# Weight splits of a decoder layer: low blocks 160 columns apart, low products placed first, second or last by block, the up projection's first high block 64 bytes up, and branch sums with a PSUM operand

## The chip, the cores and the metric

The kernel runs on one core of a Trainium2 chip. The metric is the device time of one execution in microseconds; lower is better. The kernel before took 432.97 us (median of 3 runs, 432.74 to 433.79). A core has TensorE for matrix products (PE in the profile, with its weight loads listed apart as PEld), VectorE (DVE), ScalarE (ACT), GpSimd (POOL) and SyncE (SP, which here only starts transfers). Operands lie in an on-chip memory of 128 partitions (SBUF), and TensorE writes its sums to eight banks of PSUM.

## The reference

One layer of a causal decoder for 256 tokens of width 1024, in float32. Three attention mixers (A: sparse with an indexer, B: dilated windows, C: blocks) share one input projection. Then their outputs are gated and merged, and a feed-forward block follows:

```python
gates = sigmoid(x @ w_gate).reshape(bsz, s_len, 3, D_MODEL)
merged = (gates[:, :, 0] * (o_a @ w_br_a)
          + gates[:, :, 1] * (o_b @ w_br_b)
          + gates[:, :, 2] * (o_c @ w_br_c))
x = layer_norm(ALPHA * x + merged @ w_out, ln1_g, ln1_b)
h = square(relu(x @ w_up)) @ w_down
ple = sigmoid(x @ w_ple_gate) * (p @ w_ple)
x = layer_norm(ALPHA * x + h + ple, ln2_g, ln2_b)
```

## The kernel before, in words

**Three products for one.** Every weight block and every activation is held as a pair: a high part rounded to the type fp32r, and a low part, which is the rest. A product of 128 by 128 weights with an activation is made of three matmuls into the same sum: high weight with high activation, high weight with low activation, low weight with high activation. `prod` (L154) issues them. Its argument `low` says where the matmul with the low weight stands: 0 is first, 1 is second, 2 is last. Each of the three matmuls loads its own weights.

**The stream of weights.** `Weights` (L58) takes all weights in one fixed order of units. A unit is up to 128 by 1024 floats (eight blocks of 128 columns). `_split` (L73) starts its transfer into a `raw` buffer (SP queue), copies it to the high tile `whi` with the rounding (ACT, L86), and subtracts to get the low tile `wlo` (L94). For the first 58 units VectorE makes the first 640 of each 1024 columns of `wlo` and GpSimd the others (`DV`); later VectorE makes all. There are five buffers each of `raw`, `whi` and `wlo`, and `get` (L98) keeps the split four units ahead of its use. `whi` and `wlo` are tiles of 1152 floats, and a unit may lie some columns into its tile: `at` gives the offsets. For gate and feature units the high part begins at column 40; of the low part the first five blocks begin at column 72, and the last three sit 32 columns closer (offset 40). `Apart` (L48) is the view with that one cut; the subtraction is cut at the same column. For the up projection the high part begins at 0, the first low block at 64, the others from 208 on.

**The stages.** First the indexer's features; then features (`feat`, L288), gates (`fill("g")`, L265) and values fill the matrix engine between the steps of attention, one head after the other (`head`, `slots`, `attend`). A gate or feature unit is one `gemm` (L164): 24 matmuls of 256 columns, for the eight blocks k = 0 to 7. There `low` is 2 for k = 0 to 4 and 0, 1, 2 for k = 5, 6, 7. From the last mixer on, `fill("c")` also computes the branch products of mixers B and C from `op`, which holds the attention outputs: five blocks, 15 matmuls of 256 columns, always with the low one last. The sums of both branches lie side by side in one PSUM bank (512 columns); L285 multiplies both by the gates into `G`, and L286 adds the two halves. `freed` names the instruction after which the bank counts as read. Then `merge` (L608) does the A branch: four units `u_ba` of six blocks, low last. Then come the output projection, the first norm with the gate of `p`, the up projection, the down projection and the second norm.

**The up projection.** L837 to L875: 32 units. In each, eight matmuls of 512 columns with the high blocks (L847: high and low activation side by side as one moving operand), then eight of 256 columns with the low blocks (L849). Its results go through a reduction on VectorE (L831), two ScalarE steps and a split.

**The order.** The pool layout puts `xh` and `xl` (the activation of the layer's input), `op`, `x1` (the input of the up projection) and the weight tiles at fixed bytes of each partition. The small tile `gap` (L314) only shifts `op`. The order of instructions on each engine is set when the program is built, by a list scheduler that works with modelled times, and partly by hand (`pin`, `issue_after`, `high_priority`).

Of the kernel before, what the change touches and what calls it, by code (L numbers as in the profile page):

```python
# [11 lines left out]
F32 = mybir.dt.float32  # L12
F32R = mybir.dt.float32r
ALU = mybir.AluOpType
# [25 lines left out]
FIRST = 4  # L40
DV = 640
# [5 lines left out]

class Apart:  # L48

    def __init__(self, t, cut, front, back):  # L50
        self.t, self.cut, self.at = t, cut, (front, back)

    def __getitem__(self, key):
        o = self.at[key[1].start >= self.cut]
        return self.t[:, o + key[1].start:o + key[1].stop]


class Weights:  # L58
# [14 lines left out]
    def _split(self, u):  # L73
        nc = self.nc
        src, n, hi, lo, r, by, _, at = self.units[u]
        if callable(src):
            r = src()
        elif r is None:
            r = self.raw.tile([128, 1024], F32, name="raw", tag="raw")[:, :n]
        if not callable(src):  # L80
            self.loads.append(nc.sync.dma_start(r, src).ins)
        if hi is None:
            hi = self.part.tile([128, 1152], F32R, name="whi", tag="whi")[:, at[0]:at[0] + n]
            lo = self.part.tile([128, 1152], F32R, name="wlo", tag="wlo")
            lo = Apart(lo, *at[2:], at[1]) if len(at) > 2 else lo[:, at[1]:at[1] + n]
        self.copies.append(nc.scalar.copy(hi, r).ins)  # L86
        cut = ((nc.vector, slice(None)),) if by == "v" else (
            (nc.vector, slice(0, by * n // 1024)), (nc.gpsimd, slice(by * n // 1024, n)))
        if len(at) > 2:
            o = at[2]  # L90
            cut = [(e, slice(a, b)) for e, c in cut for a, b in (
                (c.start or 0, min(c.stop or n, o)), (max(c.start or 0, o), c.stop or n)) if a < b]
        for e, c in cut:
            i = e.tensor_tensor(lo[:, c], r[:, c], hi[:, c].bitcast(F32), op=ALU.subtract)  # L94
        self.subs.append(i.ins)
        self.parts[u] = (hi, lo)

# [16 lines left out]
def hybrid_layer(ctx: ExitStack, tc: tile.TileContext, x0, xn, pT, wqk, wva, wvb, wg, wbc, wba,  # L114
                 wout, wup, wdn, wpg, wple, lnrow, rel, onehot, pick, out):
    nc = tc.nc
    pe, act, dve, pool = nc.tensor, nc.scalar, nc.vector, nc.gpsimd
# [9 lines left out]
    W = Weights(tc, raw, part)  # L127
# [20 lines left out]
    t = banks.tile([128, 512], F32, name="b4", tag="b4")  # L148
# [5 lines left out]
    def prod(ps, a, b, first, last, hold=False, more=False, low=2):  # L154

        terms = [(0, 0), (0, 1)]
        terms.insert(low, (1, 0))
        for n, (x, y) in enumerate(terms):
            i = pe.matmul(ps, lhsT=a[x], rhs=b[y], start=first and n == 0, stop=last and n == 2,  # L159
                          skip_group_check=more)  # L160
            if hold and n == 0:
                pin(i)

    def gemm(ps, units, xs, k=0):  # L164

        for u in units:
            hi, lo = W.get(u)
            for o in range(0, hi.shape[1], 128):
                prod(ps, (hi[:, o:o + 128], lo[:, o:o + 128]), xs[k], k == 0, k == len(xs) - 1,
                     low=(k - 5) if k > 4 else 2)  # L170
                k += 1


# [1 line left out]
    pm = mid.enter_context(tc.tile_pool(name="pm", bufs=1))  # L175
    one = ctx.enter_context(ExitStack())
    right = lambda n, b: one.enter_context(tc.tile_pool(name=n, bufs=b, side="right"))
    p1, k1, kp = (right(n, b) for n, b in (("p1", 1), ("k1", 2), ("kp", 3)))
# [3 lines left out]
    xs = [(xh[:, k], xl[:, k]) for k in range(KT)]  # L182
    n_u = [0]

    def add(*a, at=(0, 0)):
        i = n_u[0]
        n_u[0] += 1
        return W.add(*a, by=DV if i < 58 else "v", at=at)

    G = pm.tile([128, 24, S], F32, name="G")  # L190
    u_q = [[] for _ in range(FIRST)]

    u_g, u_bc, u_ba, u_out = [], [], [], []
    for t in TASKS:
        if t == "va":
            u_va = [add(wva[i], 656) for i in range(4)]
        elif t == "vb":
            u_vb = [add(wvb[i], 768, at=(56, 56)) for i in range(4)]
        elif t in "gcao":
            u, w, n = {"g": (u_g, wg, 1024), "c": (u_bc, wbc, 640), "a": (u_ba, wba, 768),  # L200
                       "o": (u_out, wout, 1024)}[t]
            u.append([add(w[len(u)], n, at=(0, 0) if t == "o" else (40, 72, 640, 40) if t == "g" else (40, 40))])
        else:
            u_q.append([add(wqk[int(t) - FIRST], 1024, at=(40, 72, 640, 40))])

    def toeplitz(h0, step):
        t = tp.tile([128, 3, 256], F32, name="T", tag="T")
# [29 lines left out]
    def freed(*ins):  # L237


        if banks_first[0]:  # L240
            W.after = tuple(i.ins for i in ins)
        return ins[0].ins
# [22 lines left out]
    def fill(what):  # L265


        for w in what:
            if w == "g":
                ps = mmbank(256)  # L270
                gemm(ps, u_g[n_g[0]], xs)
                freed(act.activation(G[:, n_g[0]], ps, AF.Tanh, scale=0.5))
                n_g[0] += 1
                continue
            f = n_c[0]
            n_c[0] += 1
            hi, lo = W.get(u_bc[f][0])
            ps = mmbank(512).rearrange("p (i s) -> p i s", i=2)
            for i, (k0, k1) in enumerate(((3, 5), (5, 8))):
                for k in range(k0, k1):  # L280
                    c = slice((k - 3) * 128, (k - 2) * 128)
                    prod(ps[:, i], (hi[:, c], lo[:, c]), (op[:, k, 0], op[:, k, 1]), k == k0,
                         k == k1 - 1)
            g = G[:, 3 * f + 1:3 * f + 3]
            freed(dve.scalar_tensor_tensor(g, g, 1.0, ps, op0=ALU.add, op1=ALU.mult))  # L285
            dve.tensor_tensor(g[:, 0], g[:, 0], g[:, 1], op=ALU.add)  # L286

    def feat(f):  # L288
        ps = mmbank(256)
# [21 lines left out]

    V = p1.tile([128, 2, 11, 128], F32R, name="V")
    iw = p1.tile([128, 2, 8], F32, name="iw")
    pm.tile([128, 24], F32, name="gap")  # L314
    op = pm.tile([128, 8, 2, S], F32R, name="op")

    def values(units, n, h0, heads, withiw):
# [109 lines left out]
    with ExitStack() as begin:  # L427
# [6 lines left out]
        cut = [((0, 384), (384, 768)) if k == 0 else ((0, 768),) for k in range(KT)]  # L434
        with tc.high_priority(offset=1000):
            for k in range(KT):
                for i, (a, b) in enumerate(cut[k]):
                    e = nc.scalar if i else nc.sync
                    e.dma_start(g0[:, k, a:b], x0[k, :, a:b])
            for k in range(KT):  # L440
                act.copy(xh[:, k], g0[:, k, 0:S])
                for a, b in cut[k]:
                    a = max(a, S)
# [12 lines left out]
    ps = feat(4)  # L456
# [37 lines left out]
    for j in range(2):  # L494
        ps = feat(5 + 4 * j)
        k = k_pair(ps)
# [6 lines left out]
        o = opair()  # L503
# [11 lines left out]
    for j in range(3):  # L515
        ps = feat(13 + 2 * j)
        k = k_pair(ps)
        q = q_pair(feat(14 + 2 * j))
        s = logits(k, q)
        o = opair()  # L520
        for h in range(2):
            n = 2 * j + h
# [10 lines left out]
    for j in range(3):  # L533
        s = logits(kA, q)
        o = opair()
        for h in range(2):
            n = 2 * j + h
# [23 lines left out]
    u_out += [add(wout[4 + i], 1024, wo[:, i, 0], wo[:, i, 1]) for i in range(4)]  # L561
    u_ple = [add(wple[i], 1024) for i in range(2)]
    u_pg = [add(wpg[i], 1024) for i in range(8)]
    u_up = [[add(wup[i], 1024, at=(0, 80, 128, 64))] for i in range(32)]

    H = (slice(0, 512), slice(512, 1024))

    class Wide:
# [3 lines left out]
        def __init__(self, units, stat, cut=(H, H)):  # L572
            self.units, self.stat, self.cut, self.ws = units, stat, cut, {}
            self.acc = [[next(ps_a) for _ in H] for _ in range(2)]
# [33 lines left out]
    def merge(p):  # L608
        hi, lo = W.get(u_ba[p][0])
        ps = mmbank(512).rearrange("p (f s) -> p f s", f=2)  # L610
        for f in range(2):
            for k in range(3):
                c = slice((3 * f + k) * 128, (3 * f + k + 1) * 128)
                prod(ps[:, f], (hi[:, c], lo[:, c]), (op[:, k, 0], op[:, k, 1]), k == 0, k == 2)
        g6 = G[:, 6 * p:6 * p + 6].rearrange("p (f i) s -> p f i s", f=2)
        g = g6[:, :, 0]
        dve.scalar_tensor_tensor(g, g, 1.0, ps, op0=ALU.add, op1=ALU.mult)
        dve.tensor_tensor(g, g, g6[:, :, 1], op=ALU.add)
        for f in range(2):
            o = 8192 + 512 * (2 * p + f)  # L620
            m = store[:, o:o + 512].rearrange("p (a s) -> p a s", a=2)
            act.mul(m[:, 0], g[:, f], 0.5)
            dve.scalar_tensor_tensor(m[:, 1], g[:, f], 0.5, m[:, 0].bitcast(F32), op0=ALU.mult,
                                     op1=ALU.subtract)
            mt.append(m)
# [84 lines left out]
    for i in range(4):  # L710
# [3 lines left out]
        b, cs = i // 2, H[i % 2]  # L714
        t = slice(b * 128, (b + 1) * 128)
        ps = mmbank(512)
# [62 lines left out]
    hT, at, room = {}, 0, 0  # L779
    for k in (*SEQ, *LATE):  # L780
        i = PAIRS.index(k) if k in PAIRS else -1
        n = 512 if i < 0 else 1792
        if i in (0, 1):
            t = p2.tile([128, 2048], F32R, name=("X", "PL")[i], tag=("X", "PL")[i])[:, 0:n]
        elif i in (2, 3) or k == 2:
            t = more[:, room:room + n]
            room += n
        else:
            t = store[:, at:at + n]
# [31 lines left out]
    for k in (*SEQ, *LATE):  # L821
        if k in PAIRS:
            i = PAIRS.index(k)
# [13 lines left out]
    for f in range(32):  # L837
# [5 lines left out]
        ps = mmbank(512).rearrange("p (b a t) -> p b a t", b=2, a=2)  # L843
        hi, lo = W.get(u_up[f][0])
# [15 lines left out]
        j = half_of[f].index(f)  # L860
# [47 lines left out]
    for k in SEQ[:-2]:  # L908
# [16 lines left out]
    v = w2.tile([128, D], F32, name="a8", tag="a8")  # L925
# [15 lines left out]
    for i, acc in enumerate(ends):  # L941
        c = slice(256 * i, 256 * i + 256)
# [28 lines left out]
    for b in range(2):  # L971
        t = slice(128 * b, 128 * b + 128)
# [109 lines left out]
```

## Time and profile before

| | |
|---|---|
| median of 3 runs | 432.97 us (432.74 to 433.79) |
| the profiled execution | 433.55 us; span in the trace 431.4 us |
| three kinds of matmul with `xh` or `xl` at L159 | 336 each, 279 to 281 ns from start to end |
| L847 and L849 | 256 each, 392 and 276 ns |
| high copies, L86 on ACT | 124 of raw tiles, 123.3 us |
| low subtractions, L94 | DVE 137.2 us, POOL 76.3 us |

The profile gives the time of one execution seen by the hardware profiler. The duration of a matmul is longer than the distance to the next one, since matmuls run into each other; what counts for TensorE is the distance from start to start. In the chain of waits a row has the start, the length and the number of instructions, so length by count is that distance where nothing else lies between. In the groups of instructions, a row gives busy time and mean duration, then the idle time of the engine before them.

### The profile page before, as it was taken

To read this page: it belongs to the slowest core of one execution; us is meant where nothing else is said; L and a number is where in the kernel's file an instruction comes from. 1 tells how busy PE (TensorE), PEld (TensorE's weight loads), DVE (VectorE), ACT (ScalarE), POOL (GpSimd) and SP (SyncE) were. 2 spreads that over 40 slices of the span, in tenths; PEclk is the share of its full clock that TensorE was granted. 3 is DMA by queue.
4 is the path that set the end of the run, shared out by engine and by line. 5 is a ranking of instruction groups with operands and counts; after the bars stand their busy time and mean duration, and the time that the engine had idled before them with its cause. 6 is when DMAs were issued, how large, how long until landed. Compare 5 with 4: busy or idle time off the path is not lost.

```text
span 431.4 us, 7768 instructions
## 1 busy us (share of the span) xinstructions
PE 420.4 (97%) x2804; PEld 380.4 (88%) x2804; DVE 350.5 (81%) x637; ACT 276.4 (64%) x499; POOL 123.1 (29%) x127
## 2 busy tenths in 40 slices
PE   8999999999999999999999999999999999999993
PEld 8989989999999999999887888888888888888883
DVE  4959967686576689989957878999898789999755
ACT  6777366586787785757605566887788755667310
POOL 1658246365534559400000003222530000000001
PEclk9999999999999999999999999999999999999998
DMA  8895976577554427478860677686576287647402
GB/s 292 300 327 133 257 241 195 165 224 233 161 164 131 129 74 213 121 219 330 276 259 13 216 266 206 191 289 195 173 214 193 65 286 236 183 158 231 159 2 97
DMA packets 28155, 84.28 MB, mean 195 GB/s; under 512 B 2977, under 2 KB 6985, under 8 KB 27733
## 3 DMA queue, kind: packets, MB, share of 16 engines
q1 hardware_dynamic: 26880, 79.54, 57.0%
q10 hardware_dynamic: 1140, 4.19, 3.1%
q8 instruction: 22, 0.36, 0.4%
q14 instruction: 17, 0.13, 0.1%
q0 software_dynamic: 96, 0.06, 0.0%
HBM read 81.88 MB, written 1.90 MB: 194 GB/s over the span
## 4 chain that ended last, share of the span: by engine, by line
PE 79%; DVE 8%; issue 3%; ACT 1%; POOLq 0%; DVEq 0%; POOL 0%
PE mm L159 30%; PE b L159 25%; PE mm L847 14%; PE mm L849 7%; DVE wlo L94 2%; PE b L306 2%; PE b L347 1%; DVE idx L474 1%; PE b L351 1%; DVE idx L484 1%; DVE G L285 1%; DVE G L286 1%; DVE m L483 0%; DVE eb L396 0%; DVE e L375 0%
## 5 line engine op out<-in xcount | busy, mean ns | idle before, releaser
L94 DVE TENSOR_TENSOR wlo<-raw,whi 128x640 fp32r<-128x640 f32 (+7 forms) x156 | 137.2, 903 | 24.0 <-ACT whi L86 21.8
L86 ACT CAST whi<-raw 128x1024 fp32r<-128x1024 f32 (+3 forms) x124 | 123.3, 1003 | 47.9 <-PE b L159 18.3
L94 POOL TENSOR_TENSOR wlo<-raw,whi 128x384 fp32r<-128x384 f32 (+3 forms) x58 | 76.3, 1326 | 78.0 <-ACT whi L86 75.1
L159 PE MATMUL mm<-xh,whi 128*128 128x256 f32 x336 | 92.7, 281 | 0.2 <-DVE k L260 0.2
L159 PE MATMUL mm<-xl,whi 128*128 128x256 f32 x336 | 92.0, 279 | 0.0
L159 PE MATMUL mm<-xh,wlo 128*128 128x256 f32 x336 | 87.4, 280 | 0.0
L159 PEld LDWEIGHTS mm<-xh,whi 128*128 128x128 f32 x336 | 63.1, 188 | 1.1 <-DVE k L260 0.4
L847 PE MATMUL mm<-x,whi 128*128 128x512 f32 x256 | 64.0, 392 | 0.0
L159 PEld LDWEIGHTS mm<-xl,whi 128*128 128x128 f32 x336 | 63.1, 188 | 0.5
L159 PEld LDWEIGHTS mm<-xh,wlo 128*128 128x128 f32 x336 | 60.1, 188 | 0.3
L159 PE MATMUL b<-whi,store 128*128 128x512 f32 x168 | 54.0, 389 | 0.0
L847 PEld LDWEIGHTS mm<-x,whi 128*128 128x128 f32 x256 | 45.8, 188 | 8.3
L664 POOL TENSOR_TENSOR rs<-rs,half 128x1 f32<-128x1 f32 x4 | 3.4, 841 | 147.1 <-DVE rs L663 147.1
L159 PEld LDWEIGHTS b<-whi,store 128*128 128x128 f32 x168 | 31.5, 188 | 6.5
L849 PEld LDWEIGHTS mm<-x,wlo 128*128 128x128 f32 x256 | 33.8, 188 | 2.5
L849 PE MATMUL mm<-x,wlo 128*128 128x256 f32 x256 | 34.3, 276 | 0.0
L159 PE MATMUL b<-wlo,store 128*128 128x512 f32 x84 | 32.7, 390 | 0.0
L159 PE MATMUL mm<-op,whi 128*128 128x256 f32 x128 | 23.4, 283 | 0.0
L870 POOL TENSOR_TENSOR a<-a 128x128 f32<-128x128 f32 x7 | 4.5, 640 | 60.4 <-ACT a L833 54.9
L159 PE MATMUL b<-whi,x 128*128 128x512 f32 x64 | 20.5, 395 | 0.0
L159 PEld LDWEIGHTS mm<-op,whi 128*128 128x128 f32 x128 | 19.6, 189 | 0.4 <-DVE G L285 0.3
L159 PEld LDWEIGHTS b<-wlo,store 128*128 128x128 f32 x84 | 15.8, 188 | 3.3
(219 smaller groups left out, 794.2 us busy)
## 6 DMA issues: line engine op xcount, KB each, us to landing
raw<-in_wup_dram SPq DMA_DIRECT2D x32, 512.0 KB
raw<-in_wg_dram SPq DMA_DIRECT2D x24, 512.0 KB
raw<-in_wqk_dram SPq DMA_DIRECT2D x18, 512.0 KB
raw<-in_wdn_dram SPq DMA_DIRECT2D x18, 512.0 KB
raw<-in_wout_dram SPq DMA_DIRECT2D x8, 512.0 KB
raw<-in_wpg_dram SPq DMA_DIRECT2D x8, 512.0 KB
T<-tabd SPq DMA_DIRECT2D x24, 128.0 KB
xr<-in_wdn_dram SPq DMA_DIRECT2D x6, 512.0 KB
```

Of the source, the lines that this page charges most:

```text
L86: self.copies.append(nc.scalar.copy(hi, r).ins)
L94: i = e.tensor_tensor(lo[:, c], r[:, c], hi[:, c].bitcast(F32), op=ALU.subtract)
L159: i = pe.matmul(ps, lhsT=a[x], rhs=b[y], start=first and n == 0, stop=last and n == 2, skip_group_check=more)
L285: freed(dve.scalar_tensor_tensor(g, g, 1.0, ps, op0=ALU.add, op1=ALU.mult))
L286: dve.tensor_tensor(g[:, 0], g[:, 0], g[:, 1], op=ALU.add)
L306: m = pe.matmul(ss[2 * n + h][:, QC[b]], lhsT=q[d, x, c], rhs=k[d, y, 0:128 * (b + 1)], start=i == 0, stop=i == 2)
L347: pe.transpose(t[:, 128 * i:128 * i + 128], P[:, 128 * i:128 * i + 128], ident)
L351: pe.matmul(v, lhsT=V[:, 0, vh], rhs=pt[:, :, 0:256], start=True, stop=False)
L474: dve.scalar_tensor_tensor(idx[:, QC[1]], r[:, h, QC[1]], iw[:, 1, n:n + 1], idx[:, QC[1]], op0=ALU.mult, op1=ALU.add)
L847: pe.matmul(ps, lhsT=hi[:, c], rhs=x1[:, :, k], start=k == 0, stop=False)
L849: pe.matmul(ps[:, :, 0], lhsT=lo[:, c], rhs=x1[:, :, k, 0], start=False, stop=k == KT - 1)
L870: pool.tensor_tensor(sums[2], a11, a21, op=ALU.subtract)
```

## The change

Low blocks get offsets of their own (tables `LOW` and `UP`), the tiles become 1088 floats for `whi` and 1216 for `wlo` (together as before), and `Apart` becomes a view by a list of offsets. Its `runs` finds stretches with an even step, and each stretch is one instruction with a pattern of blocks of 128 columns. In a gate or feature unit the first five low blocks are 160 columns apart, the last three 128. Branch units of mixers B and C get five blocks at 40, 200, 360, 520 and 648; VectorE makes three of the blocks and GpSimd two (before, 400 and 240 columns). Units of the A branch get six blocks 160 apart. `TURN` says for each block where the low matmul stands. In the up projection the first high block moves to column 16 and the others begin at 192, so the high copy on ACT becomes two instructions (256 and 768 columns), and the low subtraction, two instructions before too (128 and 896), is now cut at 256. `gap` grows by 32 floats. In `fill("c")` the product with the gate is made in two instructions, one for each half; the second mixer's half goes back to PSUM, and the sum then reads one operand from PSUM; the bank is now freed by the sum.

```diff
 class Apart:
-    def __init__(self, t, cut, front, back):
-        self.t, self.cut, self.at = t, cut, (front, back)
+    def __init__(self, t, at):
+        self.t, self.at = t, at
     def __getitem__(self, key):
-        o = self.at[key[1].start >= self.cut]
-        return self.t[:, o + key[1].start:o + key[1].stop]
+        o = self.at[key[1].start // 128]
+        return self.t[:, o:o + 128]
+    def runs(self, a, b):
+        i, end = a // 128, b // 128
+        while i < end:
+            j = i + 1
+            while j < end and self.at[j] - self.at[j - 1] == self.at[i + 1] - self.at[i]:
+                j += 1
+            yield 128 * i, 128 * j
+            i = j
+    def view(self, a, b):
+        i, n = a // 128, (b - a) // 128
+        step = self.at[i + 1] - self.at[i] if n > 1 else 128
+        t = self.t[:, self.at[i]:self.at[i] + n * step]
+        return t.rearrange("p (k c) -> p k c", c=step)[:, :, 0:128]
...
-            hi = self.part.tile([128, 1152], F32R, name="whi", tag="whi")[:, at[0]:at[0] + n]
-            lo = self.part.tile([128, 1152], F32R, name="wlo", tag="wlo")
-            lo = Apart(lo, *at[2:], at[1]) if len(at) > 2 else lo[:, at[1]:at[1] + n]
-        self.copies.append(nc.scalar.copy(hi, r).ins)
+            hi = self.part.tile([128, 1088], F32R, name="whi", tag="whi")
+            lo = self.part.tile([128, 1216], F32R, name="wlo", tag="wlo")
+            hi, lo = (t[:, o:o + n] if isinstance(o, int) else Apart(t, o)
+                      for t, o in zip((hi, lo), at))
+        for a, b in hi.runs(0, n) if isinstance(hi, Apart) else ():
+            i = nc.scalar.copy(blocks(hi, a, b), blocks(r, a, b))
...
+            for x in lo.runs(c0, c1):
+                i = e.tensor_tensor(blocks(lo, *x), blocks(r, *x), blocks(hi, *x).bitcast(F32),
+                                    op=ALU.subtract)
...
-                     low=(k - 5) if k > 4 else 2)
+                     low=TURN["g"][k])
...
+    LOW = {"g": (8, 168, 328, 488, 648, 776, 904, 1032), "c": (40, 200, 360, 520, 648),
+           "a": (40, 200, 360, 520, 680, 840)}
+    TURN = {"g": (0, 2, 1, 2, 2, 0, 1, 2), "c": (2, 0, 2, 1, 2), "a": (2, 1, 2, 2, 2, 0)}
...
-                         k == k1 - 1)
+                         k == k1 - 1, low=TURN["c"][k - 3])
             g = G[:, 3 * f + 1:3 * f + 3]
-            freed(dve.scalar_tensor_tensor(g, g, 1.0, ps, op0=ALU.add, op1=ALU.mult))
-            dve.tensor_tensor(g[:, 0], g[:, 0], g[:, 1], op=ALU.add)
+            for i, o in ((1, ps[:, 1]), (0, g[:, 0])):
+                dve.scalar_tensor_tensor(o, g[:, i], 1.0, ps[:, i], op0=ALU.add, op1=ALU.mult)
+            freed(dve.tensor_tensor(g[:, 0], g[:, 0], ps[:, 1], op=ALU.add))
...
-    pm.tile([128, 24], F32, name="gap")
+    pm.tile([128, 56], F32, name="gap")
...
-    u_up = [[add(wup[i], 1024, at=(0, 80, 128, 64))] for i in range(32)]
+    UP = (16, *range(192, 1088, 128)), (64, *range(208, 1104, 128))
+    u_up = [[add(wup[i], 1024, at=UP)] for i in range(32)]
...
-                prod(ps[:, f], (hi[:, c], lo[:, c]), (op[:, k, 0], op[:, k, 1]), k == 0, k == 2)
+                prod(ps[:, f], (hi[:, c], lo[:, c]), (op[:, k, 0], op[:, k, 1]), k == 0, k == 2,
+                     low=TURN["a"][3 * f + k])
```

More of the change, by code (lines that the diff above doesn't have):

```diff
@@ L48, with blocks @@
 class Apart:
-    def __init__(self, t, cut, front, back):
-        self.t, self.cut, self.at = t, cut, (front, back)
+    def __init__(self, t, at):
+        self.t, self.at = t, at
     def __getitem__(self, key):
-        o = self.at[key[1].start >= self.cut]
-        return self.t[:, o + key[1].start:o + key[1].stop]
+        o = self.at[key[1].start // 128]
[13 more added lines that the diff above has]
+        return t.rearrange("p (k c) -> p k c", c=step)[:, :, 0:128]
+def blocks(t, a, b):
+    return (t.view(a, b) if isinstance(t, Apart) else
+            t[:, a:b].rearrange("p (k c) -> p k c", c=128))
 class Weights:
@@ L82, in _split @@
         if hi is None:
-            hi = self.part.tile([128, 1152], F32R, name="whi", tag="whi")[:, at[0]:at[0] + n]
-            lo = self.part.tile([128, 1152], F32R, name="wlo", tag="wlo")
-            lo = Apart(lo, *at[2:], at[1]) if len(at) > 2 else lo[:, at[1]:at[1] + n]
[L86 to L94, printed above, removed]
+            hi = self.part.tile([128, 1088], F32R, name="whi", tag="whi")
[4 more added lines that the diff above has]
+            i = nc.scalar.copy(blocks(hi, a, b), blocks(r, a, b))
+        if not isinstance(hi, Apart):
+            i = nc.scalar.copy(hi, r)
+        self.copies.append(i.ins)
+        c = n if by == "v" else by * n // 1024
+        for e, c0, c1 in ((nc.vector, 0, c), (nc.gpsimd, c, n)):
+            if not isinstance(lo, Apart):
+                if c0 < c1:
+                    x = slice(c0, c1)
+                    i = e.tensor_tensor(lo[:, x], r[:, x], hi[:, x].bitcast(F32),
+                                        op=ALU.subtract)
+                continue
+            for x in lo.runs(c0, c1):
+                i = e.tensor_tensor(blocks(lo, *x), blocks(r, *x), blocks(hi, *x).bitcast(F32),
+                                    op=ALU.subtract)
         self.subs.append(i.ins)
@@ L183, in hybrid_layer, with add @@
     n_u = [0]
-    def add(*a, at=(0, 0)):
+    def add(*a, at=(0, 0), by=DV):
         i = n_u[0]
         n_u[0] += 1
-        return W.add(*a, by=DV if i < 58 else "v", at=at)
+        return W.add(*a, by=by if i < 58 else "v", at=at)
+    LOW = {"g": (8, 168, 328, 488, 648, 776, 904, 1032), "c": (40, 200, 360, 520, 648),
+           "a": (40, 200, 360, 520, 680, 840)}
+    TURN = {"g": (0, 2, 1, 2, 2, 0, 1, 2), "c": (2, 0, 2, 1, 2), "a": (2, 1, 2, 2, 2, 0)}
     G = pm.tile([128, 24, S], F32, name="G")
@@ L201, in hybrid_layer @@
                        "o": (u_out, wout, 1024)}[t]
-            u.append([add(w[len(u)], n, at=(0, 0) if t == "o" else (40, 72, 640, 40) if t == "g" else (40, 40))])
+            u.append([add(w[len(u)], n, at=(40, LOW[t]) if t in LOW else (0, 0),
+                          by=615 if t == "c" else DV)])
         else:
-            u_q.append([add(wqk[int(t) - FIRST], 1024, at=(40, 72, 640, 40))])
+            u_q.append([add(wqk[int(t) - FIRST], 1024, at=(40, LOW["g"]))])
     def toeplitz(h0, step):
```

## The prediction

> **What bounds the kernel now.** I read the page first (engines, then the chain that ended last), then the chain in order of time, then the starts of TensorE's instructions.
>
> ```profile
> span 431.4 us, 7768 instructions
> PE 420.4 (97%) x2804; PEld 380.4 (88%) x2804; DVE 350.5 (81%) x637; ACT 276.4 (64%) x499; POOL 123.1 (29%) x127
> PEclk9999999999999999999999999999999999999998
> PE 79%; DVE 8%; issue 3%; ACT 1%; POOLq 0%; DVEq 0%; POOL 0%
> ```
>
> TensorE is busy for 97% of the span at the full clock, and 79% of the chain is its own work. So the time is the number of matmuls by the distance from one to the next. The change removes no matmul. It can gain only if that distance, or a wait of TensorE, gets shorter. The distance is not one number:
>
> ```profile
> 77.34 4.08 PE mm L159 x36
> 112.88 4.43 PE mm L159 x39
> 187.62 14.70 PE mm L159 x125
> 253.71 1.81 PE mm L847 x8
> 255.52 0.91 PE mm L849 x8
> 256.43 1.84 PE mm L847 x8
> 258.27 0.91 PE mm L849 x8
> ...
> 338.83 1.84 PE mm L847 x8
> 340.67 0.91 PE mm L849 x8
> ```
>
> All L159 rows here are matmuls of 256 columns at the same clock. 36 in 4.08 us is 113.3 ns each, 39 in 4.43 us is 113.6, but 125 in 14.70 us is 117.6. In the up projection the first unit takes 256.43 - 253.71 = 2.72 us; the other 31 go from 256.43 to 341.58 (340.67 + 0.91), 2.747 us each. The 0.03 us lies in the eight wide matmuls (1.84 for 1.81), none in the narrow ones. So there are two paces, and the starts show where they change:
>
> ```profile
> 29.73 0.28 PE L159 MATMUL mm<-xh,whi 128*128 128x256 f32 x1
> ...
> 42.45 0.28 PE L159 MATMUL mm<-xh,wlo 128*128 128x256 f32 x1
> ...
> 141.81 0.40 PE L159 MATMUL mm<-op,whi 128*128 128x256 f32 x2
> ...
> 189.46 0.28 PE L159 MATMUL mm<-xh,whi 128*128 128x256 f32 x1
> 189.57 0.28 PE L159 MATMUL mm<-xh,wlo 128*128 128x256 f32 x1
> 189.69 0.28 PE L159 MATMUL mm<-xl,whi 128*128 128x256 f32 x1
> ...
> 190.14 0.40 PE L159 MATMUL mm<-op,whi 128*128 128x256 f32 x2
> ...
> 190.73 0.28 PE L159 MATMUL mm<-op,wlo 128*128 128x256 f32 x1
> ...
> 196.03 0.28 PE L159 MATMUL mm<-op,wlo 128*128 128x256 f32 x1
> ...
> 202.03 0.28 PE L159 MATMUL mm<-op,wlo 128*128 128x256 f32 x1
> ```
>
> From 189.46 to 190.14 six steps take 113 ns each; from 190.73 to 196.03 45 steps take 117.8 each. The pace stays as it is until something flips it. I call 113 ns the short step and 117.8 the long step. I went through the starts of all dense steps up to the end of the branch products: of 964 with `xh` or `xl`, 342 take 116 ns or more (first at 29.73, last at 189.46); of 186 with `op`, 140 (first at 141.81, last at 202.03). A long step costs 4.45 ns more (117.83 against 113.38 on average), so 1.5 us and 0.6 us are lost.
>
> What flips it? Eleven times a stretch of long steps reaches block 6 of a `gemm`, where the low matmul stands second (first at 42.45, last at 189.57); ten times it is over two steps later. From short to long it goes at transposes and other products of attention, and at every one of the three entries into `op` that come with short steps (141.81 and 190.14 are the first and the last).
>
> The layout explains the last point. In the program before, all `whi` and `wlo` buffers begin at 192 bytes modulo 256, `xh` and `xl` at 160, `op` at 32, `x1` at 192. A high block (column 40) lies 64 bytes below `xh` and 64 above `op`, modulo 256. The low blocks 0 to 4 lie like the high ones; the blocks 5 to 7, around which long steps end, lie 128 bytes off. Modulo 128 every load of these products is 64 from the moving operand. In the up projection the wide matmuls run at 0 and the narrow ones at 64; the exception is the first high block, which is loaded beside the last narrow matmul at 0. The wide matmuls after it are the longer ones. In the first unit, which comes after wide ones, they aren't.
>
> **The change part by part.** *First high up block.* At column 16 it lies 64 bytes from `x1`, so the load beside a narrow matmul has the distance of all others there, and the load of the next block beside a wide one has 0, as now. If that ends the loss, 31 units lose 27 ns each: 0.83 us. I take 0.8; the lower bound is nothing, and below nothing if the step from 64 to 0 then comes one matmul too early: at most 27 ns again, +0.8 us.
>
> *Order and low blocks.* With the new sizes (4352 and 4864 bytes) all buffers still begin at 192 modulo 256. The new low offsets put blocks 0, 2, 4, 5, 6 and 7 of a gate unit 128 bytes off the high ones, and `TURN` has the low matmul second at blocks 2 and 6, first at 0 and 5. Each of these sits on an offset of the kind at which long steps end now, at 5 and 6. The strong kind (second) comes twice in 24 steps, once before. Then a long stretch that a product of attention has begun lasts some 5 steps, not some 12: an estimate from the places in the cycle. I take 60% of the 342 long steps as gone: 205 by 4.45 ns, 0.9 us. Bounds: 0 to 1.5 us.
>
> *`op` 128 bytes further.* Now it lies to the weights as `xh` does, so the entry has no flip, and `TURN` for the branch units has a second-place low matmul as well. I take 75% of 140: 0.45 us. Bounds: 0 to 0.6 us; the loss below nothing that both edits could bring is the last rival.
>
> The rule that speaks against all this: the Trainium skill, "TensorE: Matmul & The Clock Gate", section "Back-to-back issue gap", makes the warm distance a function of the columns alone (N / 2.4 + 2.5 ns, by which 256 columns are 109 ns, an estimate). The trace disagrees: 113.3 and 117.8. By the rule the sum would be 0.
>
> *The cost on the other engines.*
>
> ```profile
> 254.00:342.00 88.00, 88.00 (x514) 77.25 (x513) 80.15 (x127) 68.55 (x121) 21.63 (x28) 1.00 0.62 187
> ...
> L86 ACT CAST whi<-raw 128x1024 fp32r<-128x1024 f32 x104 | 108.1, 1049 | 47.1 <-PE b L159 18.3 <-PE mm L159 9.2 <-DMA raw<-in_wqk_dram 7.6
> L86 ACT CAST whi<-raw 128x768 fp32r<-128x768 f32 x8 | 6.6, 830 | 0.3 <-issue 0.3
> L360 ACT CAST op<-o 128x256 fp32r<-128x256 f32 x8 | 3.2, 404 | 0.7 <-DVE o L357 0.7
> L249 DVE SCALAR_TENSOR_TENSOR q<-mm,q 128x256 fp32r<-128x256 f32 x12 | 4.9, 411 | 2.7 <-ACT q L248 2.7
> L260 DVE TENSOR_TENSOR k<-mm,k 128x256 fp32r<-128x256 f32 x5 | 2.1, 415 | 0.2
> L285 DVE SCALAR_TENSOR_TENSOR G<-G,mm x8: 669/672/679, 156.6 to 194.5; 128x512 f32<-128x512 f32 x8
> L286 DVE TENSOR_TENSOR G<-G x8: 404/416/1241, 161.0 to 196.2; 128x256 f32<-128x256 f32 x8
> L286 DVE TENSOR_TENSOR G<-G 128x256 f32<-128x256 f32 x8 | 5.1, 639 | 0.0
> L617 DVE SCALAR_TENSOR_TENSOR G<-G,mm 128x512 f32<-128x512 f32 x4 | 2.7, 679 | 0.0
> L703 DVE TENSOR_TENSOR x<-mm,x 128x512 fp32r<-128x512 f32 x3 | 2.0, 688 | 2.4 <-ACT x L699 2.4
> L727 DVE SCALAR_TENSOR_TENSOR b<-Y,PL 128x512 f32<-128x512 f32 x4 | 2.7, 695 | 0.0
> L726 DVE SCALAR_TENSOR_TENSOR PL<-sg,PL 128x512 f32<-128x512 f32 x4 | 2.6, 686 | 0.0
> L94 POOL TENSOR_TENSOR wlo<-raw,whi 128x384 fp32r<-128x384 f32 x42 | 60.7, 1452 | 62.4 <-ACT whi L86 59.6 <-PE mm L159 2.8
> L869 POOL TENSOR_TENSOR a<-a 128x128 f32<-128x128 f32 x7 | 4.2, 595 | 0.5
> PE b L351 <- DVE pt L349: 1.0, 2, 0.7
> ```
>
> The split high copy in the up projection: 404 + 830 - 1049 = 185 ns for each of 32 units, 5.9 us of ScalarE. It has 68.55 us of 88 busy there (fourth engine column), so 74.5 after; TensorE (first column, 88.00) waits for nothing in this stretch, since the split runs four units ahead. Cost 0; with the lead used up it would be up to 5.9 us. The low subtraction stays two instructions. Writing in blocks costs VectorE next to nothing: L703 writes four blocks of 128 with gaps in 688 ns, L617 a dense 512 in 679. For GpSimd no row shows blocks: between nothing and three separate instructions of 128 columns for one of 384 (3 x 595 - 1452 = 333 ns a unit), and within the lead of four units that is hidden. I take 0, by the row of VectorE, which is nearest.
>
> The branch sum: 672 + 416 becomes 411 + 411 + 415 = 1237 ns by these rows, 149 more at the median; that one of them writes to PSUM adds 9 at most (L727 to PSUM 695, L726 to SBUF 686). But L286 reads both operands from SBUF and takes up to 1241 where GpSimd works beside it; its mean is 639, by which the two were 1312 and get 75 shorter. The Trainium skill, "SBUF — State Buffer", section "SBUF: two separate sides", says that a VectorE instruction with two SBUF inputs and a GpSimd one that reads SBUF exclude each other for a whole instruction; L286 agrees. The bank is freed after 1.24 us and not 0.67; with three banks in turn and a gate unit of 24 steps between, the next use is over 2 us away: hidden. Behind the trio on VectorE wait the splits of attention: the waits of TensorE for `pt` (two, 1.0 us) can move by some tenths either way. I take 0, and ±0.5 us.
>
> Sum: -0.8 - 0.9 - 0.45 = -2.15 us against the profiled execution's own 433.55 us (span 431.4): 431.4 us. The median of the runs is 0.58 lower, 432.97, so 430.8 us.
>
> **The rivals.** *Only the up projection gains.* What ends a long stretch may be the wait for a new unit or the whole pattern of blocks 5 to 7, and spreading it does nothing. For: those blocks also differ in layout. Against: ten of eleven end within the block. Time: 432.97 - 0.8 = 432.2 us. *No pace changes*: long steps come from what else runs at the time, so neither layout nor order moves them; 433.0 us. For: long stretches mostly begin at products of attention. Against: they end at the same matmul again and again. The rule of "TensorE: Matmul & The Clock Gate" in the Trainium skill, that columns alone count, would give this too. *Slower: the mixed offsets make short steps long.* Low blocks alternate between two distances in every unit; each entry to `op` shows that a change of distance by 128 bytes can flip the pace. If that holds inside a unit, the 622 + 46 steps that are short now become long: 668 by 4.45 ns, +3.0 us, less 0.8: 435.2 us. From 472 more long steps on, net, (1.3 + 0.8 us by 4.45 ns) the kernel is slower by 0.3%. Against: blocks 5 to 7 mix both now and mostly stay short.
>
> **How the numbers follow.** Forecast 64%, only the up projection 15%, no pace change 8%, mixed offsets 13%. About 0.3%, 1.3 us, is what a measurement here can tell from no change. The forecast case spans 429.5 (all 2.95 us and half a us of waits gained) to 432; I put 4 of its 64 within 1.3 us. So faster 0.60, same 0.15 + 0.08 + 0.04 = 0.27, slower 0.13. The range reaches up to 433.4, to take in the two cases without effect with a few tenths for waits and a new order from the scheduler, and leaves out the last rival.
>
> **What would show it.** Right: all 32 up units at 2.72 us, with 1.81 for the wide half; stretches of `op` products at 113.4 ns; far fewer than 482 long steps, and each long stretch ending at a low matmul in second place; the matmul count unchanged; ACT some 6 us busier in the up projection without a wait of TensorE. Wrong: 1.84 in the up units; long stretches that pass block 2; stretches that begin inside a unit, without a product of attention before; or new waits of TensorE for VectorE near the branch sums, above 1 us together.

## The result and the profile after

The changed kernel took 431.1 us (median of 5 runs), the kernel before 433.13 us beside it: ratio 0.9943 (95% interval 0.9923 to 0.9963), 0.57% faster. The forecast was 430.8 us. The profiled execution took 430.17 us with a span of 428.4 us; before it was 433.55 and 431.4.

The page of the kernel after (spans, engines, clock, shares of the chain):

```profile
span 428.4 us, 7806 instructions
...
PE 417.6 (97%) x2804; PEld 378.4 (88%) x2804; DVE 349.9 (82%) x645; ACT 279.5 (65%) x531; POOL 120.8 (28%) x127
...
PEclk9999999999999999999999999999999999999998
...
PE 82%; DMA 4%; DVE 2%; issue 2%; SPq 1%; ACT 1%; POOLq 0%; POOL 0%; DVEq 0%
```

The matmul count is still 2804 and the clock the same, yet TensorE is busy 2.8 us less (420.4 to 417.6). How much of that is a shorter distance between matmuls (pace) and how much is waiting, the starts show. The chain in order of time:

```profile
76.85 4.08 PE mm L189 x36
...
112.44 4.49 PE mm L189 x39
...
185.19 14.70 PE mm L189 x129
...
254.19 1.81 PE mm L889 x8
256.00 0.91 PE mm L891 x8
...
335.79 1.81 PE mm L889 x8
337.60 0.91 PE mm L891 x8
```

In the same 14.70 us the last stretch of `xh` and `op` products has 129 matmuls and not 125: 114.0 ns each. In the up projection all 30 units from 254.19 to 335.79 take 2.72 us each (81.60 / 30), with 1.81 us in the wide half from first to last. The starts of TensorE's instructions in the branch products:

```profile
189.29 0.28 PE L189 MATMUL mm<-op,wlo 128*128 128x256 f32 x1
...
194.51 0.28 PE L189 MATMUL mm<-op,wlo 128*128 128x256 f32 x1
```

Between these two rows lie 46 steps: 5.22 us by 46 is 113.5 ns, where before 45 steps took 117.8 each. I counted the starts as for the prediction. "Long" is a step of 116 to 124 ns (a longer one holds a wait), and the loss is the time above 113.4 ns a step (226.7 in the up projection's wide matmuls).

| | before | after | gained |
|---|---|---|---|
| long steps with `xh` or `xl` (of about 964) | 342, 1.50 us lost | 265, 1.18 us | 0.32 us |
| long steps with `op` (of about 186) | 140, 0.62 us | 16, 0.06 us | 0.56 us |
| wide matmuls, up projection | 0.82 us lost | 0.02 us | 0.80 us |

Together that is 1.68 us of the 3.0 us by which the spans differ. Of the 77 long steps with `xh` or `xl` that are gone, 66 (96 to 30) lie in the 400 matmuls from the 1301st on, from about 156 to 205 us, among the branch products; in the 764 dense steps from 22 us up to there it is 246 before and 235 after, 0.03 us. The waits of TensorE are the next place to look (engine, line, what it waited for: total us, times, longest). Of the kernel after:

```profile
PE b L346 <- DVE q L287: 0.9, 1, 0.9
PE b L491 <- ACT sh L484: 0.5, 1, 0.5
PE mm L189 <- DVE wlo L123: 0.2, 1, 0.2
```

The two waits for `pt`, 1.0 us together before, are gone; a new one for `wlo` is small. From the gaps between starts, TensorE lost 1.29 us less than before from 160 to 180 us and 0.55 us more from 140 to 160. The first feature product with `xh` starts 0.47 us earlier (16.45 for 16.93 us). I don't count this as a gain of the change: the second profile of the same changed kernel, below, starts another 0.5 us earlier, and the kernel with only `op` moved 0.8 us earlier than before. With it the sum is 2.9 of the 3.0 us; without it, 2.4.

### The profile page after: what moved, and what is told of

Same layout as the page of the kernel before. It is cut to its first block, busy times and chain, and to the rows that moved or that the text cites. A ratio compares the mean times of both kernels' runs of the same rounds, so it can differ in the third digit from the quotient of the medians.

```text
span 428.4 us, 7806 instructions
## 1 busy us (share of the span) xinstructions
PE 417.6 (97%) x2804; PEld 378.4 (88%) x2804; DVE 349.9 (82%) x645; ACT 279.5 (65%) x531; POOL 120.8 (28%) x127
## 4 chain that ended last, share of the span: by engine, by line
PE 82%; DMA 4%; DVE 2%; issue 2%; SPq 1%; ACT 1%; POOLq 0%; POOL 0%; DVEq 0%
PE mm L189 32%; PE b L189 25%; PE mm L889 14%; PE mm L891 7%; DMA tabd<-tab 2%; DMA T<-tabd 2%; PE b L346 2%; PE b L387 1%; SPq L247 1%; PE b L391 1%; DVE eb L436 0%; PE b L392 0%; DVE st L699 0%; DVE wlo L123 0%; PE mm L740 0%
## 5 line engine op out<-in xcount | busy, mean ns | idle before, releaser
L112 ACT CAST whi<-raw 128x1024 fp32r<-128x1024 f32 (+3 forms) x92 | 89.8, 989 | 39.0 <-PE b L189 14.3
L123 DVE TENSOR_TENSOR wlo<-raw,whi 128x256 fp32r<-128x256 f32 (+3 forms) x118 | 92.9, 810 | 16.4 <-ACT whi L112 13.2
L189 PE MATMUL mm<-xh,whi 128*128 128x256 f32 x336 | 90.2, 279 | 0.0
L189 PE MATMUL mm<-xl,whi 128*128 128x256 f32 x336 | 88.4, 280 | 0.0
L123 POOL TENSOR_TENSOR wlo<-raw,whi 128x384 fp32r<-128x384 f32 (+1 forms) x50 | 69.1, 1393 | 68.3 <-ACT whi L112 66.4
L189 PE MATMUL mm<-xh,wlo 128*128 128x256 f32 x336 | 80.8, 281 | 0.2 <-DVE k L298 0.2
L189 PEld LDWEIGHTS mm<-xh,wlo 128*128 128x128 f32 x336 | 57.8, 188 | 0.9 <-DVE k L298 0.4
L119 DVE TENSOR_TENSOR wlo<-raw,whi 128x1024 fp32r<-128x1024 f32 (+2 forms) x38 | 44.2, 1185 | 5.2 <-ACT whi L112 4.8
L110 ACT CAST whi<-raw 128x256 fp32r<-128x256 f32 x64 | 36.8, 618 | 10.0 <-PE mm L889 5.4
L189 PE MATMUL mm<-op,whi 128*128 128x256 f32 x128 | 22.4, 280 | 0.0
```

The lines of the kernel that those rows point to most:

```text
L110: i = nc.scalar.copy(blocks(hi, a, b), blocks(r, a, b))
L112: i = nc.scalar.copy(hi, r)
L119: i = e.tensor_tensor(lo[:, x], r[:, x], hi[:, x].bitcast(F32), op=ALU.subtract)
L123: i = e.tensor_tensor(blocks(lo, *x), blocks(r, *x), blocks(hi, *x).bitcast(F32), op=ALU.subtract)
```

## The experiments

Theory: three layout effects set the pace (up projection, entry to `op`, order of the low blocks) and the branch sums are neutral. Rivals: the up projection alone, or no pace at all. After the first experiments the question became what the order does and what the sums do.

**The up projection's tables alone** (before, with the new `UP` and the two copies):

```
+    UP = (16, *range(192, 1088, 128)), (64, *range(208, 1104, 128))
+    u_up = [[add(wup[i], 1024, at=UP)] for i in range(32)]
```

> The kernel before with the new up projection alone (first high block at column 16, the others from 192 on, the high copy in two instructions). Theory (distance 64 for loads beside narrow matmuls, 0 beside wide ones): all 32 units take 2.72 us, 1.81 for the wide half, and the time is 0.8 us under the kernel before. Rival (the first block's place doesn't matter): units stay at 2.747 us and the time stays within 0.3 us, or the second copy instruction costs something and it is longer.

Measured 432.34 us, ratio 0.9966 (0.9950 to 0.9983). Its chain:

```profile
256.56 1.81 PE mm L887 x8
258.37 0.91 PE mm L889 x8
259.28 1.81 PE mm L887 x8
```

Units of 2.72 us; the loss there fell from 0.82 us to nothing (-0.01), while the long steps elsewhere stayed (334 and 146). So the 0.8 us belong to this edit alone. The interval of the ratio (0.7 to 2.2 us) holds it.

**`op` 128 bytes further, alone** (before, one line):

```
-    pm.tile([128, 24], F32, name="gap")
+    pm.tile([128, 56], F32, name="gap")
```

> The kernel before with op 128 bytes further and nothing else. Theory (op at another place modulo 256 than xh flips the pace on each entry and exit): of the dense steps with op under 30 are long (140 before), some fewer with xh too, and the time is 0.6 us under the kernel before. Rival (what helped op was the new order within the branch units): over 100 of the op steps stay long and the time moves by under 0.2 us.

Measured 432.57 us, ratio 0.9968 (0.9947 to 0.9989). The first entry to `op`, in the starts of TensorE:

```profile
141.27 0.39 PE L159 MATMUL mm<-op,whi 128*128 128x256 f32 x2
...
141.83 0.28 PE L159 MATMUL mm<-op,wlo 128*128 128x256 f32 x1
```

Five steps (two, one, two) in 0.56 us: short, where before the same entry turned long. Of 140 long steps 61 are left. The entry no longer flips the pace, but 61 is twice what was expected (under 30): a stretch that attention has begun still lasts here. I put that down to the branch units, which have no low block 128 bytes off (an "off" block) in this kernel; no run tests that alone. The change as a whole left 16.

**Low product always last** (after, one line):

```
+    TURN = {"g": (2,) * 8, "c": (2,) * 5, "a": (2,) * 6}
```

> The changed kernel with the low matmul last in every block; the new offsets stay. Theory A, the prediction's (a low matmul in second place ends a long stretch): nothing ends one inside a unit, over 500 of the steps with xh or xl are long (265 in the changed kernel), and the time is at least 1 us over the changed kernel. Theory B (a long stretch ends where loads that lie 128 bytes off come in between the others, mostly at the second such block after the disturbance, whatever the order): 200 to 350 long steps, time within 0.4 us of the changed kernel.

Measured 431.67 us, ratio 0.9951 (0.9922 to 0.9981), with 545 long steps of `xh` and `xl` (2.68 us lost) and 148 of `op`. From about 39.9 us on it is long for more than two units:

```profile
40.60 0.28 PE L189 MATMUL mm<-xh,wlo 128*128 128x256 f32 x1
...
43.09 0.28 PE L189 MATMUL mm<-xh,wlo 128*128 128x256 f32 x1
```

21 steps in 2.49 us, 118.6 ns each.
In the changed kernel the same unit turns short at block 4:

```profile
40.80 0.28 PE L189 MATMUL mm<-xh,whi 128*128 128x256 f32 x1
...
41.39 0.39 PE L189 MATMUL mm<-xh,wlo 128*128 128x256 f32 x2
...
42.98 0.28 PE L189 MATMUL mm<-xl,whi 128*128 128x256 f32 x1
```

The five steps up to 41.39 take 118 ns each, the 14 after it 113.6. At 41.39 stand two low matmuls, that of block 4 in **last** place and that of block 5 in first. To count where stretches end, I call one ended when at least three short steps in a row follow; a single short step inside a stretch is no end. In the experiment a block that a stretch reaches ends it 3 of 168 times: the off blocks alone do almost nothing, the order is needed. Its steps lose 2.1 us more than those of the changed kernel; by the ratios it is 0.3 to 1.8 us behind (0.9951 against 0.9943 and 0.9909).

**All low blocks off, low product last and second in turn** (after; branch units cut as before, at 400 of 640):

```
+    LOW = {"g": 8, "c": 8, "a": 8}
+    TURN = {"g": (2, 1) * 4, "c": (2, 1, 2, 1, 2), "a": (2, 1) * 3}
```

> The changed kernel with all low blocks of gate, feature and branch units 128 bytes off the high ones (dense from column 8 on), the low matmul last and second in turn. Theory B: every block is then such a block, so a long stretch ends within two blocks: under 150 long steps with xh or xl (265), under 20 with op, and 0.4 to 0.7 us under the changed kernel. Rival: each change of distance also begins long stretches, so there are over 300 of them and the kernel is slower than the changed one.

Measured 431.24 us, ratio 0.9941 (0.9921 to 0.9962); 161 and 23 long steps. That is the fewest of all, 0.35 us less lost with `xh` and `xl` than after. The stretches do not end where the low matmul stands second: of those that reach block 3 or 5 (second) 0 of 12 end, of those that reach block 2, 4 or 6 (last) 11 of 22. So my reading of the places was wrong. The time isn't lower, and its waits give a reason:

```profile
PE b L345 <- DVE q L286: 1.9, 2, 1.7
...
PE b L459 <- DMA relt<-in_pick_dram: 0.8, 1, 0.8
```

The `q` wait doubled, and a transfer for the indexer came late.

**The changed kernel again** (no edit):

> The changed kernel once more, for a comparison on the same chip. All theories: 0.994 of the kernel before, some 265 long steps with xh or xl and some 16 with op, up units of 2.72 us.

Measured 430.13 us, ratio 0.9909 (0.9886 to 0.9933); 262 and 8 long steps, -0.01 us in the up projection. The steps repeat to within 0.05 us; the medians of two measurements of one kernel differ by a ratio of 0.0034. So an effect below a microsecond is read from the steps, not from the medians.

**The new order alone** (before, with `TURN` and the old offsets):

```
+    TURN = {"g": (0, 2, 1, 2, 2, 0, 1, 2), "c": (2, 0, 2, 1, 2), "a": (2, 1, 2, 2, 2, 0)}
```

> The kernel before with the new order of the low matmuls (TURN) and nothing else: the low blocks 0 to 4 lie like the high ones, 5 to 7 are 128 bytes off as before. Theory C (a long stretch ends where the low matmul of a block that is off stands one place later in its three than that of the off block before it): the off blocks 5 to 7 have the same places as before, so 320 to 360 long steps with xh or xl, 130 to 150 with op, and a time within 0.4 us of the kernel before. Theory A (a low matmul in second place ends it): block 2 ends many, under 250 long steps with xh or xl, and the A-branch units lose theirs; 1 us under the kernel before.

Measured 433.43 us, ratio 0.9989 (0.9973 to 1.0006); 317 and 145 long steps. Order without more off blocks does next to nothing; off blocks without order (the low product always last) do nothing good. In the changed kernel the two together cut the long steps among the branch products; in the attention before them its 235 are no fewer than the 221 of this kernel.

**All off, each low product one place later than the one before**, and **one place earlier** (after, `LOW` as where all low blocks are off, branch units cut at 400 of 640):

```
+    TURN = {"g": (0, 1, 2, 0, 1, 2, 0, 1), "c": (0, 1, 2, 0, 1), "a": (0, 1, 2) * 2}
```

```
+    TURN = {"g": (2, 1, 0, 2, 1, 0, 2, 1), "c": (2, 1, 0, 2, 1), "a": (2, 1, 0) * 2}
```

> The changed kernel with all low blocks of gate, feature and branch units off by 128 bytes, the low matmul first, second, last, first, second, last and so on: each one place later than the one before. Theory C: a long stretch ends within some 8 steps, under 160 long steps with xh or xl and under 25 with op. Theory A: about the same. A rival that only counts loads between (the number of steps between two off loads, which is 4, 4 and 1) has the same ends after the 4s.

> As the kernel with places one later each, but in the opposite order: last, second, first, and again, so each low matmul stands one place earlier than the one before (first to last: two later). Theory C: nothing ends a long stretch inside a unit, over 400 long steps with xh or xl, over 100 with op, 1 us or more over its opposite. Theory A (second place ends it) and a rival that any change of place ends it: under 160, and the same time as its opposite within 0.4 us.

Later: 432.98 us, ratio 0.9984 (0.9969 to 0.9999), 191 and 19 long steps. Earlier: 431.69 us, ratio 0.9953 (0.9931 to 0.9975), 368 and 33. Layout, sizes and work are the same, so the order makes 191 or 368 (with what the scheduler makes of it). In the "earlier" kernel stretches end where the place goes up from first to last (block 3: 10 of 21; block 6: 3 of 17), hardly at a step down (blocks 1, 2, 4 and 5 together: 1 of 53). But at block 0 of the next unit, where it goes up from second to last, a single step turns short and the stretch goes on: 0 of 11 end. The expectation for this kernel, over 100 long steps with `op` and a time 1 us or more over its opposite, failed: 33, and the kernel with fewer long steps is the slower one. The waits of "later" and of "earlier":

```profile
PE b L459 <- DMA relt<-in_pick_dram: 1.6, 1, 1.6
PE mm L189 <- DVE wlo L119: 1.4, 1, 1.4
PE b L345 <- DVE q L286: 0.4, 1, 0.4
PE b L390 <- DVE pt L388: 0.3, 1, 0.3
PE b L189 <- DVE wlo L119: 0.3, 1, 0.3
```

```profile
PE b L459 <- DMA relt<-in_pick_dram: 1.0, 1, 1.0
PE b L345 <- DVE q L286: 0.8, 1, 0.8
PE mm L189 <- DVE G L325: 0.6, 1, 0.6
```

4.0 us against 2.4: these 1.6 us are more than the 0.9 us that 177 fewer long steps save (1.85 - 0.94).

**All off, second and last in turn, beginning with second** (after, `LOW` as above, the branch units cut as in the change):

```
+    TURN = {"g": (1, 2) * 4, "c": (1, 2, 1, 2, 1), "a": (1, 2) * 3}
```

> A try for a better kernel: the changed one with all low blocks of gate, feature and branch units off by 128 bytes, the low matmul second and last in turn, and the split of branch units between VectorE and GpSimd as in the changed kernel. Theory C (an off block whose low matmul stands later than the one before ends a long stretch): some 160 long steps with xh or xl (262 to 265 in the changed kernel), under 25 with op, 0.4 us less in steps. Against it: the new order of instructions brings waits of its own, which were 1.0 us more in the run with these offsets and last and second in turn; then the time is that of the changed kernel or over it.

Measured 431.25 us, ratio 0.9935 (0.9913 to 0.9958); 252 and 42 long steps. The ends lie at the last places again, now blocks 1, 3, 5, 7 (19 of 46 that reach one), not at the second places (0 of 30). Some 160 long steps were expected; that the count is higher than with the mirrored order (161) isn't explained by the places alone.

**The old branch sums in the changed kernel**, and **the new sums alone in the kernel before**:

```
-            for i, o in ((1, ps[:, 1]), (0, g[:, 0])):
-                dve.scalar_tensor_tensor(o, g[:, i], 1.0, ps[:, i], op0=ALU.add, op1=ALU.mult)
-            freed(dve.tensor_tensor(g[:, 0], g[:, 0], ps[:, 1], op=ALU.add))
+            freed(dve.scalar_tensor_tensor(g, g, 1.0, ps, op0=ALU.add, op1=ALU.mult))
+            dve.tensor_tensor(g[:, 0], g[:, 0], g[:, 1], op=ALU.add)
```

> The changed kernel with the branch sums of before (one product of 512 columns, then a sum of two operands in SBUF). Theory D (the new sums take the two waits of TensorE for pt near 165 and 175 us away, since they don't queue behind GpSimd): waits of 0.8 us or more for VectorE come back between 150 and 180 us, and the time is 0.6 to 1.2 us over the changed kernel's 430.1 to 431.1. Rival (those waits went with the new order that the scheduler made of the other edits): no such waits, within 0.4 us of the changed kernel.

> The kernel before with the new branch sums alone. Theory D: the two waits for pt (1.0 us) are gone, VectorE's sums take some 1240 ns a branch unit instead of 1312, long steps as before (some 340 with xh or xl, 140 with op), and the time is 0.7 to 1.2 us under the kernel before. Rival: the waits stay or others take their place, and the time is within 0.4 us of before.

Old sums in the changed kernel: 431.85 us, ratio 0.9946 (0.9925 to 0.9967), steps as after (252 and 37 long). New sums alone: 431.57 us, ratio 0.9946 (0.9927 to 0.9965), steps as before (320 and 151). So the sums alone are worth 2.3 us by the medians (1.5 to 3.2), 1.2 us by the spans (431.4 to 430.2), and next to nothing of it is pace (0.06 us). The stretch from 160 to 180 us (columns: PE, PEld, DVE, ACT, POOL busy, with counts), in the kernels before, with new sums alone, after, and after with old sums:

```profile
160.00:180.00 20.00, 19.01 (x161) 18.01 (x160) 18.98 (x40) 12.93 (x32) 13.60 (x13) 1.00 0.58 177
```

```profile
160.00:180.00 20.00, 20.00 (x176) 19.64 (x175) 19.08 (x46) 15.05 (x36) 14.16 (x14) 1.00 0.64 211
```

```profile
160.00:180.00 20.00, 20.00 (x179) 19.62 (x178) 18.32 (x45) 14.28 (x34) 14.18 (x14) 1.00 0.61 209
```

```profile
160.00:180.00 20.00, 18.36 (x161) 17.79 (x161) 18.35 (x40) 13.03 (x33) 14.58 (x13) 1.00 0.57 177
```

With the old sums TensorE stands for 1.0 or 1.6 us and does 161 instructions in this time; with the new ones it never stands and does 176 or 179. The waits of the changed kernel with old sums name what it waits for:

```profile
PE b L390 <- DVE pt L388: 1.6, 1, 1.6
PE b L345 <- DVE q L287: 1.4, 1, 1.4
```

VectorE's instructions in the kernel before show the queue ahead of one such wait:

```profile
164.23 0.90 DVE L286 TENSOR_TENSOR G<-G 128x256 f32<-128x256 f32 x1
165.06 0.68 DVE L356 TENSOR_TENSOR ov<-b,ov 64x512 f32<-64x512 f32 x1
165.66 0.54 DVE L349 TENSOR_TENSOR pt<-b,pt 128x384 fp32r<-128x384 f32 x1
```

and with the new sums alone:

```profile
163.57 0.54 DVE L350 TENSOR_TENSOR pt<-b,pt 128x384 fp32r<-128x384 f32 x1
...
164.24 0.41 DVE L286 SCALAR_TENSOR_TENSOR mm<-G,mm 128x256 f32<-128x256 f32 x1
...
166.36 0.41 DVE L286 SCALAR_TENSOR_TENSOR G<-G,mm 128x256 f32<-128x256 f32 x1
166.81 0.42 DVE L287 TENSOR_TENSOR G<-G,mm 128x256 f32<-128x256 f32 x1
```

Before, a sum that took 0.90 us while GpSimd worked stood two places ahead of the `pt` split that TensorE waits for. With three short pieces the split comes 2.1 us earlier and the sum after it. Whether the shorter sum or the new order on VectorE does it, these two runs don't separate: the list scheduler orders anew with each change of a duration.

The traces show what the sums are worth within the whole. From the start of the 1301st matmul to that of the 1701st TensorE takes 50.82 us before, 49.46 with the new sums alone, 50.23 after with old sums, and 48.87 after, in both of its profiles. So the new sums save 1.36 us there, alone and in the changed kernel alike; what the medians show beyond that for the sums alone isn't in these traces.

**The whole high part of the up projection at column 16** (after, one copy):

```
-    UP = (16, *range(192, 1088, 128)), (64, *range(208, 1104, 128))
+    UP = 16, (64, *range(208, 1104, 128))
```

> The changed kernel with the whole high part of an up unit at column 16, so that all its loads lie 64 bytes (modulo 128) from the moving operand, and the high copy is one instruction again. Theory (beside a wide matmul a load must lie at 0 modulo 128): the wide half takes 1.84 us or more, and the time is at least 0.7 us over the changed kernel. Rival (only the first block mattered): 1.81, the same time or less with one copy fewer.

Measured 432.99 us, ratio 0.9982 (0.9959 to 1.0006). Its chain:

```profile
256.77 1.86 PE mm L889 x8
258.63 0.94 PE mm L891 x8
259.57 1.86 PE mm L889 x8
```

A unit takes 2.80 us, 0.08 more than after, 2.5 us over 31 units; by the ratios it is 1.7 to 3.2 us behind. All 256 wide matmuls are long now (1.46 us lost), and the narrow ones, whose loads lie as before, take 117 ns each: the pace carried over. Loads 64 bytes from the moving operand (modulo 128), which nearly all short 256-column matmuls of this kernel have, spoil the 512-column ones here; there 0 is the good distance. The change puts each load at the distance of the matmul that it is loaded beside.

## Why the prediction was right, and where its terms were not

**Up projection, -0.8: right.** 0.80 us by the starts, 2.72 us for each unit as predicted, and 0.83 us by the experiment with this edit alone (0.82 to -0.01). The copies cost what the rows said (of the kernel after, groups by shape):

```profile
L110 ACT CAST whi<-raw 128x768 fp32r<-128x768 f32 x32 | 26.6, 832 | 0.0
L110 ACT CAST whi<-raw 128x256 fp32r<-128x256 f32 x32 | 12.9, 403 | 10.0 <-PE mm L889 5.4 <-PE b L189 4.2
L123 POOL TENSOR_TENSOR wlo<-raw,whi 128x384 fp32r<-128x384 f32 x42 | 61.0, 1463 | 60.0 <-ACT whi L112 58.1 <-PE b L392 1.8
```

832 and 403 ns for 830 and 404. ScalarE is busy 71.71 us of the 88 from 254 to 342 (68.55 before; I had said 74.5), TensorE 88.00, so the cover held. I had the extra work too high because I added durations: the second copy starts before the first one's record ends, and the pair takes 1.14 us from first start to last end (median of the 32), 0.09 us more than one copy and not 0.185. GpSimd's three blocks cost 11 ns, not up to 333.

**`op`, -0.45: right**, 0.56 us, and for the first reason given: the placement alone took 140 to 61. The rest took the off blocks together with the order; with the low product always last there are 148 again.

**Order and low blocks, -0.9: the step that failed.** 77 long steps went, 0.32 us, not 205 and 0.9 us, and nearly all of them among the branch products; in attention the gain is 0.03 us. I put the strong place at "second", because block 6 ended ten of eleven stretches before. In the changed kernel block 2 (second, off) ends 2 of the 13 stretches that reach it, so they pass block 2, the sign of being wrong that I had named, and block 4 (last, off) ends 9 of 15. Before, stretches mostly ended at blocks 4 to 6 as well, so in attention they last about as long. A trait that most ends share: an off low block whose low matmul stands at a later place than that of the off block before it (before: 6 after 5; after: 4 after 2; "earlier": 3 after 2 and 6 after 5). With the place unchanged hardly any end. It is no full rule: block 2 after, second behind first, hardly ends any, block 0 of "earlier" none; and before, 9 of the 21 stretches that reach block 4, which isn't off, end there, and 8 of the 15 that reach block 5, whose low matmul stands first. Before and after share one more thing there, untested alone: the low matmul of block 4 is last and that of block 5 first, so two follow each other. What TensorE does there stays open; no row shows it. The rival of mixed offsets fell: short steps stayed short at them.

**Waits, 0 ± 0.5: mis-sized.** The changed sums took the time that I gave them (1237 by the rows, 1244 measured by the means: 418 + 412 + 414), and the 1241 ns case is gone:

```profile
L325 DVE SCALAR_TENSOR_TENSOR mm<-G,mm x8: 411/418/423, 156.1 to 192.5; 128x256 f32<-128x256 f32 x8
L326 DVE TENSOR_TENSOR G<-G,mm x8: 405/413/422, 157.8 to 194.9; 128x256 f32<-128x256 f32 x8
```

(shortest, median, longest in ns.) The Trainium skill, "SBUF — State Buffer", section "SBUF: two separate sides", makes a VectorE instruction with two SBUF inputs and a GpSimd one that reads SBUF block each other. The trace agrees: with one operand in PSUM none of the 24 pieces takes over 423 ns, though 12 of them run beside a GpSimd instruction. But I called the `pt` waits able to move "by some tenths either way", and all 1.0 us of them went. I had their row before me, VectorE was busy 18.98 of the 20 us around them, and I didn't ask what stands ahead of `pt` in its queue. So 430.8 came out near 431.1 by luck: one gain was put 0.6 us too high and another about as much too low (1.29 us less waiting from 160 to 180 us, 0.55 us more before it). Removing the sums from the changed kernel makes the ratio 0.9946, against 0.9943 and 0.9909 in its two measurements, between nothing and 1.6 us; the 1.36 us of the traces lie within that.

**Columns alone don't set the distance here.** The Trainium skill, "TensorE: Matmul & The Clock Gate", section "Back-to-back issue gap", gives N / 2.4 + 2.5 ns for an isolated matmul and says that in a stream with weight loads both together set the distance, so I read its formula too widely. The place of the load does not enter there, and one kernel shows that it counts: moving seven of eight high blocks by 64 bytes (modulo 128) makes the same eight 512-column matmuls 1.86 us and not 1.81.

## What to carry to other kernels

When TensorE is full, count the start-to-start distance of equal matmuls. Two paces at one clock meant here that the place of the loads against the moving operand matters; in the up projection and at the entry to `op`, offsets alone repaired it. With a scheduler that sets the order, edits moved waits by 1 to 2 us here, so read an edit's own effect from the steps it touches, and list the waits beside it, before believing the total. Compare the same stretch of matmuls in two traces rather than the spans: the start alone moved by up to 1 us between two profiles. A VectorE instruction with two SBUF operands ahead of something that TensorE waits for is worth a try with a PSUM operand; here this was worth 1.36 us, though the means had promised 75 ns a branch unit.

## What the runs showed of the hardware

A pace of 113.4 or 117.8 ns persists over dozens of equal steps (45 long ones in a row before; more than two units, with single short steps, with the low product always last). In the up projection loads 64 bytes from the moving operand (modulo 128) go with 113.3 ns a step beside 256 columns, but beside 512 columns with 232 ns, where loads at 0 go with 226.7. On VectorE and GpSimd, writing in blocks of 128 columns with gaps cost little (GpSimd 1463 ns for 1452, VectorE 976 for 962). With one operand in PSUM a VectorE sum of 256 columns took 423 ns at most beside GpSimd, with both in SBUF up to 1241.
